# Two column halves for the small score products of a gated linear recurrence, and one address residue for three tiles

## The chip, the core and the metric

The kernel runs on one core of a Trainium2 chip. The metric is the device time of one execution in microseconds (us), the median of several runs. The core has five engines that run side by side and wait for each other through semaphores: PE (matrix products; its weight loads are shown as PEld), DVE and ACT (element-wise work and copies out of PSUM, the memory into which PE writes), POOL (element-wise work too, without access to PSUM) and SP, which here starts the transfers (DMAs).

A matrix product names a block of weights (up to 128 rows by 128 columns) and a moving block (128 rows by up to 512 columns). The number of weight columns is the number of partitions of PSUM that it writes. A product with 64 weight columns therefore writes either partitions 0 to 63 or 64 to 127; the text calls these the two column halves of the array.

## What is computed

One decoder layer on 2048 tokens of width 1024: a normalisation, a projection into two groups of heads, an output projection, a second normalisation, a gated MLP with a causal convolution of three taps, and a last normalisation. The change lies in the four heads of the first group, a linear recurrence with a decay for each channel:

```python
# S_t = diag(f_t) S_{t-1} + k_t v_t^T,  o_t = S_t^T q_t,  k_t = 1 - f_t
rel = b[:, :, :, None, :] - b[:, :, None, :, :]          # b: cumulative sum of log f
decay = jnp.exp(jnp.where(causal, rel, -jnp.inf))
scores = jnp.einsum('bhtk,bhsk,bhtsk->bhts', qi, ki, decay)
intra = jnp.einsum('bhts,bhsv->bhtv', scores, vi)
inter = jnp.einsum('bhtk,bhkv->bhtv', qi * jnp.exp(b), state)
new_state = state * jnp.exp(b_last)[...] + jnp.einsum('bhsk,bhsv->bhkv', ki * jnp.exp(b_last - b), vi)
```

The second group of heads is attention over a sliding window of 128 tokens, whose small products share PE with those of the recurrence.

## The kernel before

The tokens are worked in two halves of 1024. Each half goes through a mixing stage (heads of both groups), the output projection, gate and up projections of the MLP, and the down projection. Nearly all time goes to wide products, 128 by 128 weights on 512 columns, each of float32 data split into a high and a low part of a format that PE takes in one pass. In the trace such a product is one record. Small products of whole float32 data show as two records each (two pairs of weight load and product).

**Scores of the recurrence.** For each head, `hgrn` (L448) builds a tile `ST` of 8 chunks of 128 by 128 scores (row: the key's token s, column: the query's token t; zero unless s is not after t). It does so by levels. The diagonal (s = t) needs no decay: for each chunk one product of `K` and `q`, 128 by 128, goes to PSUM (`pdiag`, L473), four chunks to a bank, and DVE multiplies it by the identity tile `ident` on the way to `ST` (L474), which leaves the diagonal and writes zeros elsewhere. Then for m in 1, 2, 4, ..., 64 a level fills the blocks of m by m in which the query's block follows directly on the key's: keys s0 to s0+m, queries s0+m to s0+2m. Up to m = 16 one product serves two chunks and DVE copies its blocks under a mask (L502). At m = 32 and m = 64 each block is a product of its own of m by m (L515): the output starts at partition s0. At m = 32 there are two of these per chunk, at partitions 0 and 64; at m = 64 one, always at partition 0. ACT copies them into `ST` (L531), at m = 64 in one copy of 64 partitions by 8 chunks of 64.

**Output of the attention.** The products `poT` (L434) have 64 weight columns and 128 moving columns; the two heads that share a tile write partitions 0 to 63 and 64 to 127 in turn.

**The ring `ga`.** In the MLP stage two tiles with the tag `ga`, `GA` = 1056 floats wide, hold the gate's rows (1026 used). In the down projection `prep_piece` (L882) takes the same two tiles for the high and the low part of the weights of every third piece (`gad`, used at L929 to L931), and takes the ring `hi`/`lo` (4096 bytes each) for the others (`hid`, `lod`). A `ga` tile is 4224 bytes, so the second one starts 8 times 512 plus 128 bytes after the first.

**Order.** `ORDER` (L40) gives the order in which the stages are traced; a scheduler then sets the order of the instructions on each engine from its own cost estimates and from when buffers come free. So a change to one product moves others around it. Two PSUM banks with the tag `hg` are shared by `pdiag`, the levels, and the later small products of the recurrence.

Of the kernel before, what the change touches and what calls it, by code (L numbers as in the profile page):

```python
# [8 lines left out]
F32 = mybir.dt.float32  # L9
# [4 lines left out]
ALU = mybir.AluOpType  # L14
# [3 lines left out]
P = 128  # L18
# [5 lines left out]
TT = HALF // P  # L24
NB = HALF // 512
HG = 4
# [3 lines left out]
FT = FF // P  # L30
EPS = 1e-6
PIECES = [2, 2, 2, 2, 2, 1]
GA = 1056
OPS = ["B11", "T1", "B21", "T2", "T3", "B22", "T4"]
QUADS = ["A11", "A12", "A21", "A22"]
PRODUCTS = [("P1", "A11", "B11"), ("P5", "S1", "T1"), ("P6", "S2", "T2"), ("P3", "S4", "B22"),
# [13 lines left out]
def hymba_layer(ctx: ExitStack, tc: tile.TileContext, a: dict, out: bass.AP, rows_out: bass.AP):  # L50
    nc = tc.nc

    def pool(name, bufs=1, space=None, stack=ctx, **kw):
        if space is not None:
            kw["space"] = space
        return stack.enter_context(tc.tile_pool(name=name, bufs=bufs, **kw))

    cp = pool("const")
# [10 lines left out]
    def ps(kind, name):  # L69
        return spaces[kind].tile([P, 512], F32, tag=kind, name=name)  # L70
# [3 lines left out]
    def halves():  # L74
# [4 lines left out]
    nc.scalar.dma_start(nmw, a["norm_mix_w"])  # L79
    ones = cp.tile([P, P], F32, name="ones")  # L80
    nc.vector.memset(ones, 1.0)
    warm = cp.tile([P, 32], F32, name="warm")[:, 0:1]
    nc.scalar.activation(warm, ones[:, 0:1], AF.Sigmoid)
    ident = cp.tile([P, P], F32, name="ident")
    nc.gpsimd.memset(ident, 1.0)
    nc.gpsimd.affine_select(out=ident, in_=ident, compare_op=ALU.is_equal, fill=0.0,
                            base=0, pattern=[[-1, P]], channel_multiplier=1)
    state = cp.tile([P, HG, P], F32, name="state")
    halo = cp.tile([P, FT, 2], F32, name="halo")
    nc.vector.memset(halo, 0.0)  # L90
    kc = cp.tile([P, 2, P], F32R, name="kcarry")
# [172 lines left out]
    def slot(name):  # L264
        return hp.tile([P, HALF], F32, tag="m", name=name, bufs=KT)
# [52 lines left out]
    def across(t, base, dims):  # L318

        v = t[:, :]  # L320
        return bass.AP(v.tensor, v.offset + base, [list(v.ap[0])] + dims)

    def rows(kv):
        return slice(kv * HD, (kv + 1) * HD)
# [123 lines left out]
    def hgrn(hf, h, X, invb, vs, WG, gates, mix, p, fu=None):  # L448
# [8 lines left out]
        q = slot(f"hg{h}")  # L457
# [4 lines left out]
        K = p.tile([P, HALF], F32, tag="K", name="K", bufs=2)  # L462
# [3 lines left out]


        ST = p.tile([P, TT, P], F32, tag="t4", name="ST", bufs=2)
        for b in range(NB):
            pd = ps("hg", "pdiag")  # L470
            for i in range(4):
                c = slice((b * 4 + i) * P, (b * 4 + i + 1) * P)
                nc.tensor.matmul(pd[:, i * P:(i + 1) * P], K[:, c], q[:, c], start=True, stop=True)  # L473
            nc.vector.tensor_tensor(ST[:, 4 * b:4 * b + 4], pd.rearrange("p (i t) -> p i t", i=4),  # L474
                                    ident.unsqueeze(1).to_broadcast([P, 4, P]), op=ALU.mult)


        late = ORDER.index(f"p{h}") < ORDER.index(f"g{h}")
# [14 lines left out]
        for m in LEVELS:  # L493
            nb = HALF // (2 * m)
            pl = ps("hg", "plev")
            if m < 32:
                n, nu = 64 // m, TT // 2
                far, near = [[512 - m, 2], [P, nu], [2 * m, n], [1, m]], [[512 + m, 2], [P, nu], [2 * m, n], [1, m]]
                G = p.tile([P, 512], F32, tag="G", name="G", bufs=2)
                nc.scalar.copy(across(G, 0, [[m, 2], [P, nu], [2 * m, n], [1, m]]), across(K, 0, near))  # L500
                for u in range(nu):
                    marks[m] = nc.tensor.matmul(across(pl, u * 64, [[256, 2], [1, 64]]), G[:, u * P:(u + 1) * P],  # L502
                                                across(Q, u * P + m, [far[0]] + far[2:]), start=True, stop=True)
                nf = P // m
                Kv, Qv = across(K, 0, near), across(Q, m, far)
                Fk = across(F, 1, [[4 * nf - 1, 2], [nf, nu], [2, n], [0, m]])
                Fq = across(F, 0, [[4 * nf + 1, 2], [nf, nu], [2, n], [0, m]])
                nc.vector.tensor_tensor(Kv, Kv, Fk, op=ALU.mult)
                nc.vector.tensor_tensor(Qv, Qv, Fq, op=ALU.mult)
            else:  # L510
                Qv = Q.rearrange("p (b w m) -> p b w m", w=2, m=m)
                Kv = K.rearrange("p (b w m) -> p b w m", w=2, m=m)
                for c in range(TT):
                    for s0 in range(0, P, 2 * m):
                        nc.tensor.matmul(pl[s0:s0 + m, c * m:(c + 1) * m], K[:, c * P + s0:c * P + s0 + m],  # L515
                                         Q[:, c * P + s0 + m:c * P + s0 + 2 * m], start=True, stop=True)
                Fv = F.rearrange("p (b w) -> p b w", w=2)
                nc.vector.tensor_tensor(Qv[:, :, 1], Qv[:, :, 1], Fv[:, :, 0:1].to_broadcast([P, nb, m]), op=ALU.mult)
                nc.vector.tensor_tensor(Kv[:, :, 0], Kv[:, :, 0], Fv[:, :, 1:2].to_broadcast([P, nb, m]), op=ALU.mult)
            Fv = F.rearrange("p (b w) -> p b w", w=2)  # L520
            Fn = p.tile([P, max(nb, 16)], F32, tag=f"F{m}", name=f"F{m}", bufs=1)[:, 0:nb]
            nc.vector.tensor_tensor(Fn, Fv[:, :, 0], Fv[:, :, 1], op=ALU.mult)
            F = Fn
            if m < 32:
                mk = C.lmask[m].bitcast(U32).rearrange("p s t -> p (s t)")
                nc.vector.copy_predicated(across(ST.rearrange("p c t -> p (c t)"), m, far),
                                          across(mk, 0, [[64, 2], [0, nu], [m, n], [1, m]]),
                                          pl.rearrange("p (s u b m) -> p s u b m", s=2, u=nu, m=m))
                continue
            for s0 in range(0, P, 2 * m):  # L530
                nc.scalar.copy(ST[s0:s0 + m, :, s0 + m:s0 + 2 * m],  # L531
                               pl[s0:s0 + m, 0:TT * m].rearrange("p (c m) -> p c m", c=TT))
# [5 lines left out]
        for b in range(NB):  # L538
            pk = ps("hg", "pkn")
            n = min(4, kept - 4 * b)  # L540
            for i in range(n):
                c = slice((b * 4 + i) * P, (b * 4 + i + 1) * P)
# [3 lines left out]
        for b in range(NB):  # L546
            pu = ps("hg", "pu")
            for c in range(4 * b, min(4 * b + 4, kept)):
                i = c % 4
                marks["pu"] = nc.tensor.matmul(pu[:, i * P:(i + 1) * P], Kn[:, c], v[:, c], start=True, stop=True)  # L550
            for c in range(4 * b, min(4 * b + 4, kept)):
                i = c % 4
# [11 lines left out]
        for c in range(TT):  # L564
            cs = slice(c * P, (c + 1) * P)
            prev = state[:, h] if c == 0 else SS[:, c - 1]
            o = po[c // 4][:, c % 4 * P:(c % 4 + 1) * P]
# [205 lines left out]
    def gate_up(hf, ops, hs, nxt, p):  # L773
# [5 lines left out]
        for pr in range(FT // 2):  # L779
            f0 = 2 * pr  # L780
            W, nxt = nxt, None
            ga = [p.tile([P, GA], F32, tag="ga", name="ga", bufs=2)[:, 0:2 + HALF] for _ in range(2)]

# [300 lines left out]
    for hf in range(NH):  # L1084
        X, kv, invb, rs, f0 = nxt
        with ExitStack() as st:
            p = pool(f"mix{hf}", stack=st, reuse_waits="tile")
            KS, V = att_keys(hf, kv, invb, p)
            mix = [None] * KT
            vs = []  # L1090
            M, WG, gates = {}, {}, {}
            heads = [hgrn(hf, h, X, invb, vs, WG, gates, mix, p, None if h else f0) for h in range(HG)]
            pairs = [attend(hf, h, X, invb, KS, V, mix, p) for h in range(HG)]
            for name in ORDER:
                stage, n = name[:-1], int(name[-1])
                if stage in ("f", "q", "l", "s", "p"):
                    next(heads[n])
                elif stage in ("qa", "sc", "pv", "pw"):
                    next(pairs[n])
                elif stage == "g":  # L1100
                    gates[n]()
                elif stage == "w":
                    WG[n] = prep(a["w_g"][n])
                elif stage == "v":
                    vs += project_v(hf, n, X, rs, p)
                else:
                    M[n] = split(mix[n])
            M[7], M[3] = mix[7], mix[3]
        with ExitStack() as st:
            p = pool(f"ffn{hf}", stack=st, reuse_waits="tile")  # L1110
            kept, ops, hs, first = out_proj(hf, M, p)
            acts = gate_up(hf, ops, hs, first, p)
            nxt = down(hf, kept, acts, p)
# [69 lines left out]
```

## Time and profile before

| What | Before |
|---|---|
| device time, median of 3 runs | 2176.63 us (2175.63 to 2179.33) |
| the profiled execution: device time | 2176.63 us |
| the profiled execution: span, first to last instruction | 2174.6 us |
| busy share of the span: PE, PEld, DVE, ACT, POOL | 99%, 83%, 75%, 48%, 1% |
| granted clock of PE | 1.0 |
| matmul records | 11191 |

The span is 2.0 us shorter than the device time of the same execution. A row of the time line gives start and length in us, engine, source line, operation, output and inputs, shape, and how many equal instructions follow each other. Products overlap in their last part, so the length of one says little; what one costs PE is the distance from its start to the start of the next. The shape `128*64 128x64` means 128 rows by 64 weight columns, on 64 moving columns.

### The profile page before, as it was taken

The numbers are of one execution on the slowest core, as the hardware profiler recorded it, in microseconds if no ns is written. First come the engines' busy times: TensorE is split into PE (matmuls) and PEld (weight loads), VectorE is DVE, ScalarE is ACT, GpSimd is POOL, SyncE is SP. The second block draws the span as 40 slices with busy tenths as digits, with TensorE's granted clock in tenths as the row PEclk, the third lists the DMA queues.
The fourth block names the chain that finished last, engine by engine and source line by source line (L and its number), as shares of the span: only waits on it lengthen the run. The fifth ranks groups of instructions, "written<-read, shape, count | busy, mean of one in ns | idle before, by whom it ended". The sixth has DMA issues, their size and how long they took to land.

```text
span 2174.6 us, 28950 instructions
## 1 busy us (share of the span) xinstructions
PE 2158.8 (99%) x11191; PEld 1812.7 (83%) x11191; DVE 1624.5 (75%) x2429; ACT 1045.0 (48%) x1828; POOL 12.6 (1%) x37
## 2 busy tenths in 40 slices
PE   8999999999999999999999999999999999999998
PEld 7988988888888888888889889888888888888887
DVE  6566668689787888785765676677888888787865
ACT  6445455554444445345635365445644444443453
POOL 2000000000000000000000000000000000000000
PEclk9999999999999999999999999999999999999999
DMA  4111012413333234974641110114232323259743
GB/s 156 40 30 40 30 35 73 132 63 124 94 113 97 90 128 146 375 244 147 211 136 30 30 46 25 49 63 142 71 117 87 126 88 121 87 187 392 238 145 131
DMA packets 91145, 254.40 MB, mean 117 GB/s; under 512 B 11136, under 2 KB 13952, under 8 KB 91008
## 3 DMA queue, kind: packets, MB, share of 16 engines
q1 hardware_dynamic: 90576, 252.29, 34.8%
q8 instruction: 88, 1.44, 0.3%
q14 instruction: 49, 0.40, 0.1%
q10 hardware_dynamic: 432, 0.27, 0.0%
HBM read 195.37 MB, written 57.15 MB: 116 GB/s over the span
## 4 chain that ended last, share of the span: by engine, by line
PE 97%; DVE 1%; DMA 1%; ACT 1%; issue 0%; SPq 0%; DVEq 0%; ACTq 0%
PE pop L202 8%; PE X L742 7%; PE X L744 7%; PE X L743 7%; PE q L202 4%; PE hq L202 4%; PE g L202 4%; PE f L202 4%; PE Y L743 4%; PE Y L744 4%; PE Y L742 4%; PE pdx L931 3%; PE pdy L930 3%; PE pdx L930 3%; PE pdy L931 3%; PE pdx L929 3%
## 5 line engine op out<-in xcount | busy, mean ns | idle before, releaser
L617 ACT CAST whi<-raw 128x1024 fp32r<-128x1024 f32 x88 | 92.5, 1051 | 103.0 <-PE X L743 68.3
L813 DVE SCALAR_TENSOR_TENSOR y<-ga,cw,y 128x1024 f32<-128x1024 f32 x88 | 112.2, 1277 | 37.7 <-ACT y L811 37.7
L743 PE MATMUL X<-T,whi 128*128 128x512 f32 x352 | 136.9, 389 | 0.0
L742 PE MATMUL X<-T,whi 128*128 128x512 f32 x352 | 136.9, 389 | 0.0
L744 PE MATMUL X<-T,wlo 128*128 128x512 f32 x352 | 136.9, 389 | 0.0
L618 DVE TENSOR_TENSOR wlo<-raw,whi 128x1024 fp32r<-128x1024 f32 x88 | 107.0, 1216 | 5.6 <-ACT whi L617 5.6
L183 ACT CAST whi<-raw 128x1024 fp32r<-128x1024 f32 x58 | 60.5, 1048 | 98.0 <-PE g L202 20.1
L748 ACT COPY u<-X 128x512 f32<-128x512 f32 x88 | 51.6, 586 | 99.2 <-PE X L744 99.1
L618 DVE TENSOR_TENSOR xld<-raw,xhd 128x1024 fp32r<-128x1024 f32 x72 | 80.8, 1130 | 8.8 <-ACT xhd L617 8.5
L617 ACT CAST xhd<-raw 128x1024 fp32r<-128x1024 f32 x72 | 69.2, 976 | 33.7 <-DMA raw<-act0B 9.4
L202 PE MATMUL pop<-XH,wlo 128*128 128x512 f32 x256 | 83.7, 391 | 0.8 <-DVE wlo L184 0.8
L202 PE MATMUL pop<-XL,whi 128*128 128x512 f32 x256 | 83.8, 391 | 0.0
L202 PE MATMUL pop<-XH,whi 128*128 128x512 f32 x256 | 83.2, 396 | 0.2
L184 DVE TENSOR_TENSOR wlo<-raw,whi 128x1024 fp32r<-128x1024 f32 x58 | 70.2, 1215 | 12.5 <-ACT whi L183 12.5
L744 PEld LDWEIGHTS X<-T,wlo 128*128 128x128 f32 x352 | 66.1, 188 | 13.7
L743 PEld LDWEIGHTS X<-T,whi 128*128 128x128 f32 x352 | 66.1, 188 | 13.7
L742 PEld LDWEIGHTS X<-T,whi 128*128 128x128 f32 x352 | 66.1, 188 | 13.7
L748 ACT COPY s<-X 128x512 f32<-128x512 f32 x44 | 25.8, 587 | 106.5 <-PE X L744 106.5
L609 PE MATMUL pvv<-whi,XH 128*128 128x256 f32 x256 | 73.4, 288 | 0.0
L610 PE MATMUL pvv<-whi,XL 128*128 128x256 f32 x256 | 73.0, 287 | 0.0
L611 PE MATMUL pvv<-wlo,XH 128*128 128x256 f32 x256 | 72.4, 286 | 0.0
L742 PE MATMUL X<-T,Sh 128*128 128x512 f32 x176 | 68.7, 390 | 0.0
(391 smaller groups left out, 6532.1 us busy)
## 6 DMA issues: line engine op xcount, KB each, us to landing
wr<-in_w_down SPq DMA_DIRECT2D x90, 512.0 KB, 5.5
raw<-in_w_gate SPq DMA_DIRECT2D x44, 512.0 KB, 3.6
raw<-in_w_up SPq DMA_DIRECT2D x44, 512.0 KB, 3.7
raw<-act0T SPq DMA_DIRECT2D x20, 512.0 KB, 5.4
raw<-act1T SPq DMA_DIRECT2D x20, 512.0 KB, 4.9
act0B<-y SPq DMA_DIRECT2D x33, 256.0 KB, 2.3
act1B<-y SPq DMA_DIRECT2D x33, 256.0 KB, 2.2
raw<-in_w_out SPq DMA_DIRECT2D x16, 512.0 KB, 3.6
```

The lines of the kernel that those rows point to most:

```text
L202: nc.tensor.matmul(o[b], w, x[:, bs], start=f, stop=l)
L609: nc.tensor.matmul(o[:, 0:256], xh[:, t], hi[:, c], start=kt == 0, stop=False)
L610: nc.tensor.matmul(o[:, 0:256], xl[:, t], hi[:, c], start=False, stop=False)
L617: nc.scalar.copy(h, src)
L618: return (eng or nc.vector).tensor_tensor(l, src, h.bitcast(F32), op=ALU.subtract)
L742: nc.tensor.matmul(o, wh[:, ws], xh, start=i == 0 and not more, stop=False, skip_group_check=more)
L743: nc.tensor.matmul(o, wh[:, ws], xl, start=False, stop=False, skip_group_check=more)
L744: nc.tensor.matmul(o, wl[:, ws], xh, start=False, stop=i == 3, skip_group_check=more)
L748: nc.scalar.copy(t, o)
L813: nc.vector.scalar_tensor_tensor(y, g[:, w:w + HALF], C.cw[:, ft, w:w + 1], y, op0=ALU.mult, op1=ALU.add)
L930: nc.tensor.matmul(o, wh[:, i, c], al[:, i, cols], start=False, stop=False, skip_group_check=more)
L931: nc.tensor.matmul(o, wl[:, i, c], ah[:, i, cols], start=False, stop=l, skip_group_check=more)
```

## The change

Three things are changed.

1. The diagonal. A block of 64 by 64 tokens replaces the chunk of 128 by 128: 16 products per head in place of 8, each with 64 weight columns and 64 moving columns, the first half of a chunk to PSUM partitions 0 to 63 and the second to 64 to 127, in turn. All fit in one bank in place of two. DVE multiplies by the identity's two diagonal blocks, one instruction of 64 partitions by 512 for each half. The lower left quarter of each chunk, which the multiplication by the identity used to clear, is cleared by a memset on POOL.
2. Level 64. The 8 products per head write partitions 0 to 63 for even chunks and 64 to 127 for odd ones. ACT takes them out in two copies of 64 partitions by 256, the second from partitions 64 to 127 to partitions 0 to 63.
3. Addresses. `GA` becomes 1152 floats, 9 times 512 bytes, so both `ga` tiles start at the same residue of 512 bytes. `ident` and `state` are allocated ahead of the small tile `warm`. In the built program nearly all wide tiles stand at 192 bytes past a multiple of 512. Before the change, `ident` and the second `ga` tile stood at 320, the tiles `dd` and `fw` behind the ring at 448; after it all four stand at 192.

```diff
-GA = 1056
+GA = 1152
...
     nc.vector.memset(ones, 1.0)
+    ident = cp.tile([P, P], F32, name="ident")
+    state = cp.tile([P, HG, P], F32, name="state")
     warm = cp.tile([P, 32], F32, name="warm")[:, 0:1]
     nc.scalar.activation(warm, ones[:, 0:1], AF.Sigmoid)
-    ident = cp.tile([P, P], F32, name="ident")
...
-    state = cp.tile([P, HG, P], F32, name="state")
...
         ST = p.tile([P, TT, P], F32, tag="t4", name="ST", bufs=2)
-        for b in range(NB):
-            pd = ps("hg", "pdiag")
-            for i in range(4):
-                c = slice((b * 4 + i) * P, (b * 4 + i + 1) * P)
-                nc.tensor.matmul(pd[:, i * P:(i + 1) * P], K[:, c], q[:, c], start=True, stop=True)
-            nc.vector.tensor_tensor(ST[:, 4 * b:4 * b + 4], pd.rearrange("p (i t) -> p i t", i=4),
-                                    ident.unsqueeze(1).to_broadcast([P, 4, P]), op=ALU.mult)
+        nc.gpsimd.memset(ST[rows(1), :, 0:64], 0.0)
+        pd = ps("hg", "pdiag")
+        for c in range(TT):
+            for k in range(2):
+                ts = slice(c * P + k * 64, c * P + (k + 1) * 64)
+                nc.tensor.matmul(pd[rows(k), c * 64:(c + 1) * 64], K[:, ts], q[:, ts], start=True, stop=True)
+        for k in range(2):
+            r = rows(k)
+            nc.vector.tensor_tensor(ST[r, :, r], pd[r].rearrange("p (c t) -> p c t", t=64),
+                                    ident[r, r].unsqueeze(1).to_broadcast([64, TT, 64]), op=ALU.mult)
...
                 for c in range(TT):
                     for s0 in range(0, P, 2 * m):
-                        nc.tensor.matmul(pl[s0:s0 + m, c * m:(c + 1) * m], K[:, c * P + s0:c * P + s0 + m],
+                        o = pl[s0:s0 + m, c * m:(c + 1) * m] if m < 64 else pl[rows(c % 2), c // 2 * m:(c // 2 + 1) * m]
+                        nc.tensor.matmul(o, K[:, c * P + s0:c * P + s0 + m],
                                          Q[:, c * P + s0 + m:c * P + s0 + 2 * m], start=True, stop=True)
...
+            if m == 64:
+                for k in range(2):
+                    nc.scalar.copy(ST[0:m].rearrange("p (c k) t -> p c k t", k=2)[:, :, k, m:],
+                                   pl[rows(k), 0:TT // 2 * m].rearrange("p (c m) -> p c m", m=m))
+                continue
```

Since the scheduler works from the changed costs, the order on PE moves at many places of the mixing stage. Three of them show the kinds of moves. Lines of the changed kernel stand up to 9 further down (L473 becomes L474, L502 becomes L505, L515 becomes L519); `hg_533` and the like are the query tile of a head.

PE, first token half, head 0, the diagonal among the wide products `q` of the attention; before:

```order
L202 MATMUL q_657<-XL,whi 128x512
L202 MATMUL q_658<-XL,whi 128x512
L473 MATMUL pdiag<-hg_533,K 128x128 x8
L202 MATMUL q_657<-XH,wlo 128x512
L202 MATMUL q_658<-XH,wlo 128x512
```

and now:

```order
L202 MATMUL q_666<-XL,whi 128x512
L202 MATMUL q_667<-XL,whi 128x512
L474 MATMUL pdiag<-hg_533,K 64x64 x16
L505 MATMUL plev<-Q,G 128x2x64 x4
L202 MATMUL q_666<-XH,wlo 128x512
L202 MATMUL q_667<-XH,wlo 128x512
```

The first level, which stood 19 wide products further on as an interruption of its own, now follows the diagonal directly.

PE, first token half, head 2, where the diagonal meets the output products `poT` of an attention pair; before:

```order
L473 MATMUL pdiag<-hg_1920,K 128x128 x6
L434 MATMUL poT<-po,V 64x128
L434 MATMUL poT<-pp,V 64x128
L473 MATMUL pdiag<-hg_1920,K 128x128
L434 MATMUL poT<-pp,V 64x128
L434 MATMUL poT<-po,V 64x128 x2
```

and now:

```order
L474 MATMUL pdiag<-hg_1938,K 64x64 x7
L434 MATMUL poT<-po,V 64x128
L434 MATMUL poT<-pp,V 64x128
L474 MATMUL pdiag<-hg_1938,K 64x64 x2
L434 MATMUL poT<-pp,V 64x128
L434 MATMUL poT<-po,V 64x128 x2
```

The order is the same; what was an alternation of 128 and 64 weight columns is now one run of products with 64.

PE, first token half, head 3, where the diagonal meets the attention's scores `psc`; before:

```order
L473 MATMUL pdiag<-hg_2736,K 128x128 x6
L387 MATMUL psc<-KS,qh 128x128
L473 MATMUL pdiag<-hg_2736,K 128x128
L387 MATMUL psc<-KS,qh 128x256
L473 MATMUL pdiag<-hg_2736,K 128x128
L202 MATMUL g_3283<-XH,whi 128x512
```

and now:

```order
L474 MATMUL pdiag<-hg_2763,K 64x64 x8
L387 MATMUL psc<-KS,qh 128x128
L474 MATMUL pdiag<-hg_2763,K 64x64
L387 MATMUL psc<-KS,qh 128x256
L474 MATMUL pdiag<-hg_2763,K 64x64 x7
L505 MATMUL plev<-Q,G 128x2x64 x4
L202 MATMUL g_3319<-XH,whi 128x512
```

Here the narrow run is cut twice by products with 128 weight columns. The second token half has the same three pictures.

## The prediction, made before the changed kernel was run

> **What bounds the kernel now.** I read the page first: busy times, then the chain that ended last, then what PE waited for.
>
> ```profile
> span 2174.6 us, 28950 instructions
> PE 2158.8 (99%) x11191; PEld 1812.7 (83%) x11191; DVE 1624.5 (75%) x2429; ACT 1045.0 (48%) x1828; POOL 12.6 (1%) x37
> PE 97%; DVE 1%; DMA 1%; ACT 1%; issue 0%; SPq 0%; DVEq 0%; ACTq 0%
> ...
> PE kv L202 <- ACT XH L216: 6.3, 2, 5.4
> PE poT L434 <- DVE po L426: 1.0, 2, 0.5
> PE pop L202 <- DVE wlo L184: 0.8, 2, 0.4
> ```
>
> PE is busy for 99% of the span, the chain is PE for 97%, and of its waits 6.3 us lie at the start, where nothing changes; the others are of 1 us and less. So the time is the sum of what each product costs PE, plus about 8 us. A change is worth what it takes off the distance between the starts of products, wherever it stands, as long as DVE keeps up.
>
> **The price of a small product.** The time line of PE around head 0's diagonal:
>
> ```profile
> 61.13 0.61 PE L202 MATMUL q<-XL,whi 128*128 128x512 f32 x2
> 61.58 1.95 PE L473 MATMUL pdiag<-hg,K 128*128 128x128 f32 x16
> 63.28 0.71 PE L202 MATMUL q<-XH,wlo 128*128 128x512 f32 x2
> 63.83 0.62 PE L202 MATMUL q<-XH,whi 128*128 128x512 f32 x2
> 64.29 0.61 PE L202 MATMUL q<-XL,whi 128*128 128x512 f32 x2
> ```
>
> A pair of wide products takes 0.455 (61.13 to 61.58, 63.83 to 64.29). From 61.13 to 63.83 are 2.70 us with two such pairs in it, so the 16 records of the diagonal cost 1.79, or 0.112 each, and the interruption itself nothing that can be seen.
>
> Level 64 and level 32, with the wide products about them (the second row of each level is the same run, from an answer cut off earlier):
>
> ```profile
> 93.17 0.28 PE L611 MATMUL pvv<-wlo,XH 128*128 128x256 f32 x1
> 93.38 1.15 PE L515 MATMUL plev<-Q,K 128*64 128x64 f32 x16
> 94.80 0.28 PE L611 MATMUL pvv<-wlo,XH 128*128 128x256 f32 x1
> ...
> 93.38 0.56 PE L515 MATMUL plev<-Q,K 128*64 128x64 f32 x6
> ...
> 88.52 0.28 PE L609 MATMUL pvv<-whi,XH 128*128 128x256 f32 x1
> 88.73 0.70 PE L515 MATMUL plev<-Q,K 128*32 128x32 f32 x32
> 89.58 0.28 PE L611 MATMUL pvv<-wlo,XH 128*128 128x256 f32 x1
> 89.70 0.28 PE L609 MATMUL pvv<-whi,XH 128*128 128x256 f32 x1
> ...
> 88.73 0.51 PE L515 MATMUL plev<-Q,K 128*32 128x32 f32 x20
> ```
>
> Level 64, all in one column half: 10 more records take 1.15 − 0.56 = 0.59, so 0.059 each. Level 32, alternating between partitions 0 and 64: 12 more take 0.70 − 0.51 = 0.19, so 0.016 each, two in 0.032. A wide `pvv` product takes 0.12 (89.58 to 89.70). From 93.17 to 94.80 are 1.63; without three steps of 0.12 that is 1.27, of which 16 × 0.059 = 0.94 are the records. The rest, **0.33, is the price of going to narrow weights and back**; level 32 gives 1.18 − 0.36 − 0.51 = 0.31.
>
> Do two halves really run at once, with 64 columns? The output products of the attention alternate in the same way. First all of one run by a window on L434 (length, PE busy, records, then PEld), then rows of its time line:
>
> ```profile
> 131.03:132.71 1.68, 1.67 (x26) 1.50 (x26) 1.00 0.00 0
> ...
> 131.42 0.27 PE L434 MATMUL poT<-po,V 128*64 128x128 f32 x1
> 131.42 0.38 PE L434 MATMUL poT<-pp,V 128*64 128x128 f32 x2
> 131.64 0.27 PE L434 MATMUL poT<-pp,V 128*64 128x128 f32 x1
> 131.64 0.38 PE L434 MATMUL poT<-po,V 128*64 128x128 f32 x2
> ```
>
> Two records start at 131.42, two at 131.64 (and two between): two in 0.11, where one with 128 moving columns alone takes 0.112. 26 in a row would be 2.9 us; the run took 1.67. So a pair costs what one does, and I take 0.059 for a pair of 64 by 64. The bounds are 0.032 (level 32's pair, half as wide) and 0.118 (one after the other).
>
> The Trainium skill says otherwise in one place ("TensorE: Matmul & The Clock Gate", Part 3, what overlaps and what doesn't): a weight load overlaps a running product only when their row groups differ. Here all products use all 128 rows, so by that rule the halves would go in turn with the loads exposed. The `poT` rows above speak against it; it is the third rival below.
>
> **The sum**, against the profiled execution's own 2176.63 us (span 2174.6 and 2.0 around it; it is also the median of the three runs).
>
> 1. *Diagonal*: 64 products of two records, 128 × 0.112 = 14.3 us. Now 128 products, 64 pairs of products, 128 pairs of records: 128 × 0.059 = 7.6. **−6.7** (between −10.2 and +0.8).
> 2. *Level 64*: 128 × 0.059 = 7.6 becomes 64 pairs, 3.8. **−3.8** (between −5.5 and 0).
> 3. *Going narrow and back*: the diagonal was 128 wide and is now 64. Counted in PE's order before and after, runs of narrow products go from 55 to 63: heads 0 and 1 add one each, head 3 three (cut twice by `psc`), head 2 saves one net since its diagonal now joins the two `poT` runs. 8 × 0.33 = **+2.6**.
> 4. *Interruptions of the wide products*: 202 become 191 in PE's order, as the first level now stands right behind the diagonal. The interruption above cost nothing within itself; the first wide pair behind it took 0.55 in place of 0.455 (63.28 to 63.83), part of it weight load that the last small product had already given back. So between 0 and 0.1 each: **−0.5** (−1.1 to 0).
> 5. *Addresses.* The groups of the down projection, same operation and shape, by ring:
>
> ```profile
> L929 PE MATMUL pdx<-xhd,gad 128*128 128x512 f32 x96 | 37.4, 389 | 0.0
> L930 PE MATMUL pdx<-xld,gad 128*128 128x512 f32 x96 | 38.0, 395 | 0.0
> L931 PE MATMUL pdx<-xhd,gad 128*128 128x512 f32 x96 | 37.2, 397 | 0.0
> L930 PE MATMUL pdx<-xld,hid 128*128 128x512 f32 x168 | 65.4, 389 | 0.0
> L931 PE MATMUL pdx<-xhd,lod 128*128 128x512 f32 x168 | 63.4, 389 | 0.0
> L742 PE MATMUL Y<-B,dd 128*128 128x512 f32 x8 | 3.1, 389 | 0.0
> ...
> 877.73 0.39 PE L929 MATMUL pdx<-xhd,gad 128*128 128x512 f32 x1
> 881.20 0.39 PE L929 MATMUL pdx<-xhd,gad 128*128 128x512 f32 x1
> ...
> 872.07 0.39 PE L929 MATMUL pdx<-xhd,hid 128*128 128x512 f32 x1
> 875.47 0.39 PE L743 MATMUL X<-T,whi 128*128 128x512 f32 x1
> ```
>
> With `ga` weights the products at L930 and L931 are 6 and 8 ns longer than with the ring `hi`/`lo`; at L929 they are not. While L930 runs, the low part is loaded, and L931 multiplies by it: both touch the second `ga` tile, the one that stands 128 bytes off the others. The tile `dd`, 256 off, shows 389. So the offset of 128 is the suspect. In starts: 15 products from 877.73 to 881.20 take 3.47, 15 without `ga` from 872.07 to 875.47 take 3.40, so 0.0047 per product; with 96 triples in `pdx`, 80 in `pdy` and 2 × 16 with the `xh2d` operands there are 624 products: **−2.7**, estimated (0 to −3).
> The same for `ident`: 335 transposes of 128 columns, a quarter of the width, so at most about 2 ns each, 0.7 either way. I take 0.
> 6. *Off PE.* DVE: two instructions of 512 elements per partition before and now. ACT: one copy more per head; POOL: a memset per head, four times as long per partition as those of the profile:
>
> ```profile
> L474 DVE TENSOR_TENSOR ST<-pdiag,ident x16: 682/692/693, 62.7 to 1412.2; 128x512 f32<-128x512 f32 x16
> L531 ACT COPY ST<-plev x24: 344/363/581, 89.5 to 1447.4; 32x256 f32<-32x256 f32 x16, 64x512 f32<-64x512 f32 x8
> L113 POOL MEMSET lmask<- 128x128 f32 x5 | 1.0, 204 | 0.0
> ...
> 350.00:370.00 20.00, 19.16 (x170) 16.39 (x169) 17.12 (x34) 10.77 (x44) 0.00 (x0) 1.00 0.06 23
> 1420.00:1450.00 30.00, 29.07 (x228) 25.06 (x227) 27.00 (x50) 15.90 (x52) 0.00 (x0) 1.00 0.15 49
> ```
>
> Two copies of 256 at 0.36 in place of one at 0.58 are 0.14 more per head on an engine that is busy for 48%; uncovered, 1.1 in all. The memset is about 0.8 (4 × 0.204) on an idle POOL with nothing queued behind it. DVE's first masked copy into `ST` waits for it, and behind that the products `K` and `Q` of the next level; it becomes free to run with the same buffer for which DVE waited before, and PE's diagonal runs meanwhile. Uncovered it would be 6.5. I take 0 for both.
> 7. *Waits.* The last two rows (length, then busy PE, PEld, DVE, ACT, POOL) are the end of each mixing stage: DVE is busy for 17.1 of 20 and 27.0 of 30 us, and PE is short of work for 0.8 and 0.9. DVE gets no less to do there, and PE comes sooner. **+0.5** (0 to +4).
>
> −6.7 − 3.8 + 2.6 − 0.5 − 2.7 + 0.5 = −10.6: **2166.0 us**.
>
> **The rivals.**
>
> *The addresses do nothing*: the 6 and 8 ns come from something else about the ring, say its two parts lying in one tag. For it: the trace shows no address. Against it: `hid`/`lod` are loaded in the same rhythm, and only the second tile's products are slow. Without step 5: 2168.7.
>
> *DVE becomes the bound at the end of the mixing stages.* For it: the two windows. Against it: in the windows before them it has slack, and the gain of head 3, next to the end, is only a quarter of 7.9 (steps 1 to 3), 1 us per half. If PE loses all of that and as much again to a later DVE, +3 to +4 on step 7: 2169.4.
>
> *The halves do not run at once for 64 by 64, and it gets slower.* The place is each narrow run; with pairs at p, steps 1 and 2 give 192 p against 21.9. Without the addresses' help, and with +2.6 of step 3 and steps 4 and 7 cancelling, break-even is p = 19.3 / 192 = 0.100. From there on it is slower; at 0.118 it is +3.4 without step 5 (2180) and about +0.7 with it (2177.3). Against it: `poT` and level 32, which both alternate in the same way.
> By the Trainium skill's rule on row groups the loads would stand between the products too: the `poT` run's loads, 1.50 us for 26 or 0.058 each, make it 384 × 0.117 = 45 us for 21.9, and with step 3 about 2202.
>
> *More than forecast*: interruptions worth 0.1 each and no new waits, 2164.
>
> **Chances and numbers.** Forecast 0.60 (of its own 2164.5 to 2167.5); addresses nothing 0.13; DVE 0.15; more than forecast 0.05; in turn with the addresses' help, no change, 0.04; in turn and slower 0.03, the rule's case 0.01 of it. The range from 2163 to 2171 holds the first four and leaves out the two with halves in turn and the far end of the DVE case. A measurement of this kernel tells about 0.2%, 4.4 us, from no change: all of the first four are beyond that but for the DVE case's far end. Faster 0.91, same 0.06, slower 0.03.
>
> **What will show it.** Level 64's run should take about 0.61 us to the next start in place of 1.08, a diagonal run alone 1.08 in place of 1.79, with starts in pairs. Records of `gad` should all show 389. PE's waits at `poT` and level 32 at the ends of the mixing stages show step 7. I am wrong if starts come singly 0.059 apart, if PE idles for more than 4 us more at the ends of the mixing stages, or if the memset is what DVE waits for.

## The result, and the profile after

The changed kernel takes **2168.17 us** (median of 7 runs, 2167.45 to 2171.08) where the kernel before, beside it, takes 2176.01 (2175.59 to 2179.33): ratio 0.9962, 95% interval 0.9953 to 0.9972. The forecast was 2166.0, with a range from 2163 to 2171. The two profiled executions are 2176.63 and 2167.45, the spans 2174.6 and 2165.7, 8.9 us apart; the medians are 7.8 apart. Run again later, the changed kernel took 2169.77 beside 2176.32 (0.9970, 0.9958 to 0.9981).

The page of the changed kernel, its first rows, the chain and what PE waited for (us in total, times, longest):

```profile
span 2165.7 us, 29275 instructions
PE 2148.0 (99%) x11319; PEld 1801.6 (83%) x11319; DVE 1624.0 (75%) x2429; ACT 1046.9 (48%) x1836; POOL 20.7 (1%) x45
PE 97%; DVE 2%; DMA 0%; ACT 0%; issue 0%; SPq 0%; DVEq 0%; ACTq 0%
...
PE kv L202 <- ACT XH L216: 6.0, 2, 5.6
PE poT L434 <- DVE pp L426: 2.5, 3, 1.2
```

PE still sets the time, and its busy time is 10.8 us shorter with 128 more records (64 more products of two records each). What is new is the second wait: 2.5 us at `poT`, 1.0 before. DVE stands in the chain with 2% in place of 1%.

The groups that the change touches (busy us, mean ns of one, idle before):

```profile
L474 PE MATMUL pdiag<-hg,K 128*64 128x64 f32 x256 | 11.5, 226 | 0.0
L519 PE MATMUL plev<-Q,K 128*64 128x64 f32 x128 | 5.6, 227 | 0.0
L530 DVE COPY_PREDICATED ST<-lmask,plev 128x512 f32<-128x512 uint32 x40 | 38.3, 957 | 0.3
L939 PE MATMUL pdx<-xld,gad 128*128 128x512 f32 x96 | 37.3, 389 | 0.0
L940 PE MATMUL pdx<-xhd,gad 128*128 128x512 f32 x96 | 36.4, 389 | 0.0
```

The `gad` products of the last two rows, at 395 and 397 ns before, are at 389 like those at L938. DVE idles 0.3 us in all ahead of the masked copies that wait for POOL's memset, so that one is covered.

The diagonal of head 0 and its level 64 in the time line of PE (start, length to the last end, line, number of records):

```profile
60.86 0.61 PE L202 MATMUL q<-XL,whi 128*128 128x512 f32 x2
61.40 1.15 PE L474 MATMUL pdiag<-hg,K 128*64 128x64 f32 x32
62.48 0.95 PE L505 MATMUL plev<-Q,G 128*128 128x128 f32 x6
...
91.80 0.28 PE L618 MATMUL pvv<-whi,XH 128*128 128x256 f32 x1
92.01 0.69 PE L519 MATMUL plev<-Q,K 128*64 128x64 f32 x16
92.62 0.39 PE L619 MATMUL pvv<-whi,XL 128*128 128x256 f32 x1
```

From 61.40 to 62.48 are 1.08 for the whole diagonal, from 92.01 to 92.62 are 0.61 for level 64: the two numbers that the prediction named as its test.

Where the 8.9 us of the two spans lie shows a sum over the whole trace: for each product the distance from its start to the start of the next one on PE, grouped by what the product is. The table gives the difference to the kernel before in us, for the changed kernel and for four kernels that make only a part of the change (the first four experiments). A wait counts with the product that stands ahead of it.

| products | before | after | addresses alone | halves alone | diagonal alone | level 64 alone |
|---|---|---|---|---|---|---|
| diagonal | 14.28 | -4.49 | 0 | -4.49 | -4.49 | 0 |
| levels 1 to 16 | 33.02 | +1.14 | 0 | +1.14 | +1.13 | 0 |
| `poT`, `ppt` | 51.80 | -1.47 | 0 | -1.46 | -1.48 | +0.06 |
| other small, wide ones of the mixing stages | 738.6 | +0.52 | -0.15 | +0.84 | +0.49 | +0.21 |
| level 64 | 8.53 | -3.03 | 0 | -3.03 | 0 | -3.05 |
| level 32 (with the wait behind it) | 6.21 | +1.32 | 0 | +1.32 | +1.31 | 0 |
| `gad` | 144.3 | -2.73 | -2.73 | 0 | 0 | 0 |
| `kv` at the start, rest of the feed-forward | 1165.8 | -0.90 | -0.62 | -0.15 | -0.59 | -1.20 |
| all | 2162.5 | -9.63 | -3.50 | -5.85 | -3.59 | -3.99 |

The last group but one is chance: its products are the same in all six kernels, and in a second profile of the changed kernel it stood at +0.63. In that second execution PE's granted clock (the figure behind POOL) stands at 0.50 for 3.4 us of this group, and the products there cost 1.6 us more in all:

```profile
1093.90:1097.30 3.40, 3.40 (x9) 2.69 (x9) 1.96 (x14) 1.05 (x1) 0.00 (x0) 0.50 0.23 89
```

The first profiles of the six kernels have no such stretch ahead of the last product. Three later ones have it at the end of the second mixing stage, behind PE's wait at `poT`: the changed kernel with `GA` at 1088 and at 1120, and the diagonal on quarters. In the first two the group of `poT` and `ppt` is 1.0 and 1.2 us longer than in the changed kernel, with the same order of products. Apart from this the other groups repeat to 0.1 us or so, and the parts add up to within 0.2. To the span come 0.1 more at the start and 0.6 more behind the last product.

### The profile page after: what moved, and what is told of

Read it like the earlier page. It is cut to its first block, busy times and chain, and to the rows that moved or that the text cites. A ratio compares the mean times of both kernels' runs of the same rounds, so it can differ in the third digit from the quotient of the medians.

```text
span 2165.7 us, 29275 instructions
## 1 busy us (share of the span) xinstructions
PE 2148.0 (99%) x11319; PEld 1801.6 (83%) x11319; DVE 1624.0 (75%) x2429; ACT 1046.9 (48%) x1836; POOL 20.7 (1%) x45
## 3 DMA queue, kind: packets, MB, share of 16 engines
q8 instruction: 89, 1.46, 0.3%
## 4 chain that ended last, share of the span: by engine, by line
PE 97%; DVE 2%; DMA 0%; ACT 0%; issue 0%; SPq 0%; DVEq 0%; ACTq 0%
PE X L751 7%; PE X L753 7%; PE X L752 7%; PE pop L202 7%; PE q L202 4%; PE g L202 4%; PE hq L202 4%; PE f L202 4%; PE Y L753 4%; PE Y L752 4%; PE Y L751 4%; PE pdx L938 3%; PE pdx L939 3%; PE pdx L940 3%; PE pdy L939 3%; PE pdy L940 3%
## 5 line engine op out<-in xcount | busy, mean ns | idle before, releaser
L626 ACT CAST xhd<-raw 128x1024 fp32r<-128x1024 f32 x72 | 69.3, 978 | 34.9 <-DMA raw<-act0B 10.6
```

Of the source, the lines that this page charges most:

```text
L626: nc.scalar.copy(h, src)
```

## The experiments

**The parts of the change, each alone.** Four kernels between before and after. *Addresses alone* is the kernel before with these lines:

```diff
-GA = 1056
+GA = 1152
     ones = cp.tile([P, P], F32, name="ones")
     nc.vector.memset(ones, 1.0)
+    ident = cp.tile([P, P], F32, name="ident")
+    state = cp.tile([P, HG, P], F32, name="state")
     warm = cp.tile([P, 32], F32, name="warm")[:, 0:1]
     nc.scalar.activation(warm, ones[:, 0:1], AF.Sigmoid)
-    ident = cp.tile([P, P], F32, name="ident")
...
-    state = cp.tile([P, HG, P], F32, name="state")
```

> Only the addresses of the changed kernel: the second ga tile, dd and ident stand at the same residue as the first; the column halves are left as before. The theory (step 5): gad records at L930 and L931 fall from 395 and 397 to 389 ns, 624 products at 0.0047 less, 2.7 us off the kernel before (about 2173.5 where it takes 2176.2). The rival (the addresses do nothing, the 6 and 8 ns come from the rhythm of the loads and vanished with the new order of the products): the records stay at 395 and 397 and the time within 0.5 us of the kernel before.

Measured: 2173.61 (11 runs) beside 2176.36, ratio 0.9988 (0.998 to 0.9997).

```profile
L930 PE MATMUL pdx<-xld,gad 128*128 128x512 f32 x96 | 37.3, 389 | 0.0
L931 PE MATMUL pdx<-xhd,gad 128*128 128x512 f32 x96 | 36.4, 389 | 0.0
```

These are the two slow groups of `gad` in this kernel, whose order of products is that of the kernel before. Both are as fast as the others now, and the table gives 2.73 us for 624 products. The place in memory is the cause; the rival falls. The transposes by `ident`, which was moved too, stay within 0.03 us per group (`ppt`, `pkn`, `pot`): its place is worth nothing, as the prediction took it.

*Halves alone* is the changed kernel with the old `GA` and the old order of `ident` and `state`:

> Only the column halves of the changed kernel: diagonal and level 64 as in it, the addresses as before. The theory (steps 1 to 4 and 7): -6.7 - 3.8 + 2.6 - 0.5 = -8.4 on PE, of which 1 to 2 come back as waits at poT at the ends of the mixing stages: -6 to -7 against the kernel before, gad records at 395 and 397. The rival on the addresses: -8 to -9 as in the changed kernel, with gad records at 389.

Measured: 2171.84 (11 runs) beside 2176.36, ratio 0.9981 (0.9972 to 0.999); the `gad` groups show 395 and 397 again. By the medians it is 4.5, by PE's starts 5.85, short of the 6 to 7 expected.

*Diagonal alone* takes into the kernel before only the new loop at `pdiag`, its memset and its two products by `ident`; *level 64 alone* only this and the two copies that belong to it:

```diff
-                        nc.tensor.matmul(pl[s0:s0 + m, c * m:(c + 1) * m], K[:, c * P + s0:c * P + s0 + m],
+                        o = pl[s0:s0 + m, c * m:(c + 1) * m] if m < 64 else pl[rows(c % 2), c // 2 * m:(c // 2 + 1) * m]
+                        nc.tensor.matmul(o, K[:, c * P + s0:c * P + s0 + m],
```

> The kernel before with the new diagonal alone; level 64 in one half, old addresses. The theory (steps 1, 3 and 4): -6.7 + 2.6 - 0.5 = -4.6, a diagonal run that stands alone 1.08 us to the next start. A rival for the going narrow (that it costs nothing, 0 in place of 0.33 a run): -7.2. If the waits at poT come with the diagonal: up to 1.5 less gain, and the page lists 2.5 us of them as in the changed kernel.

> The kernel before with level 64 alternating between the halves alone; diagonal 128 wide, old addresses. The theory (step 2): 16 records in 0.61 us to the next start in place of 1.08, -3.8 if all of it reaches the end, since no run is added and DVE has the same to do. If DVE bounds the place where level 64 stands in heads 2 and 3: only -2 to -3, and PE's waits grow by as much.

Measured: diagonal alone 2173.51 (11 runs), ratio 0.9989 (0.998 to 0.9998); level 64 alone 2174.01 (11 runs), ratio 0.9989 (0.9981 to 0.9998). Of PE's waits, `poT` with the diagonal alone:

```profile
PE poT L434 <- DVE pp L426: 2.5, 3, 1.2
```

and with level 64 alone, with one that is new there:

```profile
PE poT L434 <- DVE po L426: 1.0, 2, 0.5
...
PE pop L202 <- ACT XH L444: 0.2, 1, 0.2
```

The new wait at `poT` comes with the diagonal, not with level 64. Level 64's own gain is smaller than 8 x 0.46: six of its runs go from 1.075 to 0.615 us to the next start, but behind the two of head 3 PE runs into a wait, in the first half one of 0.07, too short for the list (0.756 to the next start), in the second half the second row above, which leaves its run at 1.04 as before. In size that is near the second theory's case, 3.05 of 3.8, but the engine that PE waits for there is ACT and not DVE.

**Does the alternation make the pair?** The changed kernel, with the diagonal's two loops swapped:

```diff
-        for c in range(TT):
-            for k in range(2):
+        for k in range(2):
+            for c in range(TT):
                 ts = slice(c * P + k * 64, c * P + (k + 1) * 64)
```

> The changed kernel with the diagonal's two loops swapped: the same 256 records, but first all of the lower column half and then all of the upper one, so that neighbours no longer alternate. The theory (a pair of halves runs in the time of one product only because neighbours write different halves): records 0.059 apart as in level 64 of the kernel before, 256 x 0.059 = 15.1 in place of 7.6, +7.5 us against the changed kernel and about the time of the kernel before. The rival (a 64 by 64 product is cheap by itself, or the two halves go in turn anyway): a run still 1.08 us long, no change.

Measured: 2173.49 (11 runs) beside 2177.56, ratio 0.9984 (0.9975 to 0.9993). The time line of PE at the same place:

```profile
62.19 1.90 PE L474 MATMUL pdiag<-hg,K 128*64 128x64 f32 x32
64.02 0.72 PE L505 MATMUL plev<-Q,G 128*128 128x128 f32 x4
```

The same 32 records take 1.83 in place of 1.08, and the sum over the diagonals is 5.48 us higher than in the changed kernel; all other groups but the chance one stay within 0.15. So neighbours in different column halves run at once, and neighbours in one half go in turn, 0.059 each. The rule of the Trainium skill that the prediction weighed ("TensorE: Matmul & The Clock Gate", Part 3, what overlaps and what doesn't) does not hold for these products: they share all row groups, and the pair costs what one does. The table "Why this matters for your kernels" on the same page of the Trainium skill has the other side of it, small outputs put on distinct column groups to run together; that agrees with 1.08 against 1.83. The expected 7.5 was too high. A run of 32 strictly in turn would take 0.107 for its first record, 30 x 0.059, and 0.152 for its last, 2.03 in all; level 64 of the kernel before has the same two ends and 14 x 0.059 between them, 1.075. The run here takes 1.83, since near its middle, where the lower half gives way to the upper, three pairs of records start only 4 to 7 ns apart. The alternating run has the same ends: 16 x 0.059 = 0.94, and 0.14 on top.

**Which distance costs?** The changed kernel with other values for `GA`: 1040 puts the second `ga` tile 64 bytes off the first modulo 512 and `dd` 128 off, 1088 puts them 256 and 0 off, 1120 puts them 384 and 256 off.

> The changed kernel with the second ga tile 64 bytes off the residue of the first, modulo 512 (128 off before, 0 now), and dd 128 off. If any step off the residue costs the same: gad records at L939 and L940 at 395 and 397 ns. If it is the 128 itself, and dd with it: gad at 389, and dd (8 records, 256 off before and at 389) above 389. The rival, that the offset is not the cause: all 389.

> The changed kernel with the second ga tile 256 bytes off the residue of the first, modulo 512, and dd at the residue itself. By the row of dd in the kernel before, which stood 256 off and showed 389 ns: gad records at 389 throughout. If any offset but 0 costs: 395 and 397 at L939 and L940.

> The changed kernel with the second ga tile 384 bytes off the residue of the first modulo 512, dd at 256 off. After the offsets of 64 and 128 cost 2 to 9 ns per product and 256 nothing, a rule modulo 256 expects gad records at L939 and L940 at 395 and 397 ns, as for 128, and dd at 389. A rule modulo 512 of the distance alone (384 is as far as 128 from the next 512) expects the same; that only small positive offsets cost, 389 throughout.

Their groups, 64 first, with `dd`:

```profile
L939 PE MATMUL pdx<-xld,gad 128*128 128x512 f32 x96 | 37.6, 391 | 0.0
L940 PE MATMUL pdx<-xhd,gad 128*128 128x512 f32 x96 | 37.1, 397 | 0.0
...
L751 PE MATMUL Y<-B,dd 128*128 128x512 f32 x8 | 3.2, 396 | 0.0
```

256:

```profile
L939 PE MATMUL pdx<-xld,gad 128*128 128x512 f32 x96 | 37.3, 389 | 0.0
L940 PE MATMUL pdx<-xhd,gad 128*128 128x512 f32 x96 | 36.4, 389 | 0.0
```

and 384:

```profile
L939 PE MATMUL pdx<-xld,gad 128*128 128x512 f32 x96 | 38.0, 395 | 0.0
L940 PE MATMUL pdx<-xhd,gad 128*128 128x512 f32 x96 | 37.2, 397 | 0.0
...
L751 PE MATMUL Y<-B,dd 128*128 128x512 f32 x8 | 3.1, 389 | 0.0
```

64, 128 and 384 cost, 0 and 256 do not; and `dd`, a tile of quite another stage, turns slow in the one kernel where it stands 128 off. All that was seen fits a rule modulo 256. Whether the distance from the other tile counts, or the second tile's own place, no run separates: the other tiles stayed where they were. Each was run once; by PE's starts their `gad` products take 0.2, 2.7 and 0.0 us less than in the kernel before.

**Is DVE what PE waits for at the end of the mixing stage?** The time line of PE in the changed kernel, at the last head of the first half:

```profile
358.52 1.04 PE L423 MATMUL ppt<-ident,sc 128*128 128x128 f32 x8
359.49 0.70 PE L519 MATMUL plev<-Q,K 128*32 128x32 f32 x32
361.37 1.05 PE L434 MATMUL poT<-po,V 128*64 128x128 f32 x7 [1.18 <-DVE pp L426]
```

and DVE there:

```profile
358.72 0.69 DVE L512 TENSOR_TENSOR Q<-Q,F 128x512 f32<-128x512 f32 x1
359.33 0.73 DVE L530 COPY_PREDICATED ST<-lmask,plev 128x512 f32<-128x512 uint32 x1
359.95 0.68 DVE L426 TENSOR_TENSOR po<-ppt,ownT 128x512 f32<-128x512 f32 x1
360.54 0.68 DVE L426 TENSOR_TENSOR pp<-ppt,prevT 128x512 f32<-128x512 f32 x1
361.14 0.68 DVE L426 TENSOR_TENSOR po<-ppt,ownT 128x512 f32<-128x512 f32 x1
```

In the kernel before PE did the same work in another order there:

```profile
361.25 0.60 PE L423 MATMUL ppt<-ident,sc 128*128 128x128 f32 x4
361.69 1.06 PE L502 MATMUL plev<-Q,G 128*128 128x128 f32 x8
362.58 0.60 PE L423 MATMUL ppt<-ident,sc 128*128 128x128 f32 x4
363.32 0.41 PE L434 MATMUL poT<-po,V 128*64 128x128 f32 x2
363.90 0.70 PE L515 MATMUL plev<-Q,K 128*32 128x32 f32 x32 [0.17 <-DVE Q L509]
365.12 0.54 PE L434 MATMUL poT<-po,V 128*64 128x128 f32 x5 [0.52 <-DVE po L426]
```

Before, half of the transposes `ppt` stood ahead of level 16, and DVE did half of `po` and `pp` before it came to level 16's Q (363.16). Now all eight stand behind it, and DVE has Q, the masked copy and the first products by the masks to do one after the other before `poT` may start. The test takes one of these instructions away:

```diff
             if m < 32:
                 mk = C.lmask[m].bitcast(U32).rearrange("p s t -> p (s t)")
+                if h == 3 and m == 16:
+                    continue
                 nc.vector.copy_predicated(across(ST.rearrange("p c t -> p (c t)"), m, far),
```

> The changed kernel without one instruction of DVE per half: head 3's masked copy of level 16 into ST is left out, so the scores of that level are missing in head 3. PE's order is the same. The theory (at the ends of the mixing stages DVE, not PE, sets when poT can start, and part of the gain went there): the time from level 32 of head 3 to the next start falls from 1.88 us by DVE's 0.6 to about 1.28 in each half, PE's wait at poT from 2.5 to about 1.3, the time by about 1.2. The rival (PE waits for ACT's exponentials or for the transposes, DVE is only the last name on the list): no change.

Measured: 2168.30 (5 runs) beside 2177.56, ratio 0.9958 (0.9946 to 0.9971). The medians cannot tell 1.2 us from the changed kernel; the time line can:

```profile
360.00 0.70 PE L519 MATMUL plev<-Q,K 128*32 128x32 f32 x32
361.27 1.05 PE L434 MATMUL poT<-po,V 128*64 128x128 f32 x7 [0.57 <-DVE pp L426]
```

From level 32 to `poT` it is 1.27 in place of 1.88, the same in the second half, and the group of level 32 in the sum falls by 1.22. The 0.6 us of DVE ahead of `po` are 0.6 us of PE. DVE sets the start of `poT`, and the rival falls. That it is the new place of the transposes that made this wait longer, and not only that PE comes sooner, is argued from the two time lines; no run puts the old order into the changed kernel.

Behind level 64 of the same head the wait is another. The output projection `pop` starts at 364.45 in the changed kernel, where level 64 has run from 363.67; what ends just before is a cast on ACT, which could start only when `poT` was done:

```profile
363.81 0.59 ACT L444 CAST XH<-poT 128x512 fp32r<-128x512 f32 x1 [1.26 <-PE poT L434]
...
364.45 0.73 PE L202 MATMUL pop<-XH,whi 128*128 128x512 f32 x2
```

Level 64 is work that PE does meanwhile; a shorter level 64 does not bring `pop` forward. No run shortens this cast, so that part rests on the time line.

**Further in the same direction.** First the changed kernel again, for its runs on the same chip and its longer end.

> The changed kernel once more, for the runs beside it on the same chip. The theory: 8 us below the kernel before, 2168 where that takes 2176; PE's distances as in its first profile (diagonal runs 1.08, level 64 0.61, level 32 of head 3 1.88 us to the next start), the end behind the last product 7.2 to 7.3 us again. If the longer end (0.6 more than in the kernel before) was a chance of one execution: 6.7.

Measured: 2169.77 as told above; PE's groups within 0.1 us of the first profile (the last but one, `kv` and the feed-forward, 1.5 more, by the stretch at half the clock), and 7.26 us from PE's last start to the end of the span. The longer end repeats.

Then four column quarters in place of two halves, for the diagonal (blocks of 32 tokens) and for level 32:

```diff
-        nc.gpsimd.memset(ST[rows(1), :, 0:64], 0.0)
+        nc.gpsimd.memset(ST, 0.0)
...
-            for k in range(2):
-                ts = slice(c * P + k * 64, c * P + (k + 1) * 64)
-                nc.tensor.matmul(pd[rows(k), c * 64:(c + 1) * 64], K[:, ts], q[:, ts], start=True, stop=True)
+            for k in range(4):
+                ts = slice(c * P + k * 32, c * P + (k + 1) * 32)
+                nc.tensor.matmul(pd[k * 32:(k + 1) * 32, c * 32:(c + 1) * 32], K[:, ts], q[:, ts], start=True, stop=True)
...
+                        if m < 64:
+                            r0 = s0 + 32 * (c % 2)
+                            o = pl[r0:r0 + m, c // 2 * m:(c // 2 + 1) * m]
...
```

DVE then has four instructions of 32 partitions in place of two of 64, and ACT twice as many copies at level 32.

> A further step of the changed kernel: the diagonal from blocks of 32 tokens on four column quarters (64 records a run), and level 32 on four quarters where it alternated between two. The theory that column groups run at once, carried on to four: four records in the 0.032 us that two take now, 0.008 each, a diagonal run 0.43 and a level 32 run 0.25 shorter, 8 of each: -5.4 us against the changed kernel. The rival (a record is not issued faster than every 0.016 us): level 32 as before, the diagonal 64 x 0.016 = 1.02 in place of 0.94, so +0.7 us; with DVE's four smaller instructions in place of two and more narrow work between, 0 to +2.

> Only the diagonal of that further step on four quarters, level 32 left on two. By four at once: -3.4 us against the changed kernel, a run alone 0.65 in place of 1.08 us to the next start. By one record per 0.016: +0.7, a run 1.16.

Measured: quarters 2166.40 (5 runs), ratio 0.9954 (0.994 to 0.9967); the diagonal alone on quarters 2168.83 (5 runs), 0.9964 (0.9952 to 0.9977); the changed kernel beside them 0.9970. The time line of PE with quarters, diagonal and level 32 of head 0:

```profile
62.17 0.76 PE L474 MATMUL pdiag<-hg,K 128*32 128x32 f32 x64
62.86 0.83 PE L505 MATMUL plev<-Q,G 128*128 128x128 f32 x5
...
87.72 0.46 PE L523 MATMUL plev<-Q,K 128*32 128x32 f32 x32
88.10 0.39 PE L626 MATMUL pvv<-wlo,XH 128*128 128x256 f32 x1
```

64 records in 0.69 and 32 in 0.38 us to the next start (on two halves the diagonal took 1.08 and level 32 0.63): four run at once, and no limit of one record per 0.016 us shows. The diagonals give 3.0 us and level 32, with the wait behind it, another 1.9, a little less than expected (3.4 and 2.0), but the medians only 3.4. PE's waits in and behind the mixing stages grow, and here it is ACT that they name; in the changed kernel its waits for ACT other than `kv` were 0.2:

```profile
PE poT L434 <- DVE pp L426: 1.6, 2, 1.4
PE pop L202 <- ACT XH L444: 1.3, 2, 1.1
PE po L584 <- ACT on L587: 1.0, 2, 0.5
PE poT L434 <- DVE m L405: 0.9, 1, 0.9
```

The diagonal alone on quarters misses its forecast: its diagonals give the same 3.0 us, but its median lies only 0.9 below the changed kernel's, where 3.4 were expected. It has the same new waits for ACT (0.9 and 1.0), and its profile also the stretch at half the clock.

The kernel with both on quarters is the fastest of all that ran, 9.9 us below the kernel before by medians. The intervals of the two ratios overlap, but on this chip its slowest run (2167.79) is faster than the fastest of the changed kernel beside it (2168.84).

## Why the prediction held, step by step

- *Steps 1, 3 and 4, diagonal, narrowing, interruptions* (-6.7, +2.6, -0.5, together -4.6): in the kernel with the diagonal alone the first four groups of the table, which are all that they touch but for the wait, give -4.49 + 1.13 - 1.48 + 0.49 = -4.35. The sum of the three is right to 0.3, and the rival by which going narrow costs nothing (-7.2) falls; the three terms one by one no run separates. The price per pair, 0.059 for two of 64 by 64, is right: with neighbours in one half the same records go in turn.
- *Step 2, level 64* (-3.8): a run goes from 1.075 to 0.615, 0.46; eight are 3.7. PE got 3.03 of it. The 0.65 that is missing is a wait behind head 3's runs and belongs to step 7.
- *Step 5, addresses* (-2.7): -2.73, with the order of the products unchanged. It was found from three groups of the same shape that differed by 6 and 8 ns.
- *Step 6, off PE* (0): PE waits nowhere for the memset, ACT's copies or DVE's new form.
- *Step 7, waits* (+0.5): **the step that was mis-sized.** It measured +1.32 behind level 32 and +0.65 behind level 64 of head 3, +2.0 in all, about 1.0 in each half. That is the gain of head 3, which the second rival priced at 1 us per half and saw lost with as much again on top. The first part of that rival happened, the second did not, and only the 1.32 is a wait for DVE: the 0.65 is one for ACT's cast, which step 7 did not have. The prediction looked at how busy DVE is in these windows; it should have followed the chains from level 16 over DVE to `poT`, and from `poT` over ACT to `pop`, instruction by instruction, in the changed order. That the transposes now stand in one piece behind level 16 could be read from the order before the run.
- *Left out of the sum*: the end behind the last product, +0.6 (below).

So PE's sum, without the chance group, is -4.35 - 3.7 - 2.73 + 2.0 = -8.8, where the table has -8.7 and the forecast -10.6. With the chance group's -0.9, and 0.7 back at both ends, this makes the 8.9 of the two spans. By the number alone the prediction was less good than by its rows: the median of 2168.17 lies in the range but outside the forecast's own 2164.5 to 2167.5, and nearest to the 2168.7 of the rival in which the addresses do nothing, which the rows refute. Of the rivals, the one that kept the time unchanged or slower (halves in turn) is refuted by the swapped loops: in turn the diagonal alone would have cost 5.5 us more.

## What to carry to other kernels

Where PE is the bound and a product's output has at most half of the 128 columns, write neighbours into different column halves or quarters: here they ran at once, and it is the order of neighbours that decides, so an inner loop over the halves is all that it needs. Where groups of one shape differ by a few ns, compare the addresses of the weight tiles; 4.4 ns on average over 624 products were nearly a third of this gain. And when PE gets faster, add up the instructions of the next engine between what PE hands over and what it takes back, in the changed order: DVE's busy share of 86% and a cast on an ACT that is busy for 48% hid two chains that together took back a whole head's gain.

## What the runs showed that was not expected

- *The place of weight tiles*: with the second `ga` tile 64, 128 or 384 bytes off, two of the three products of `gad` cost 2 to 8 ns more each, at 256 none; `dd`, which stood 0, 128 and 256 off, was slow at 128 alone. What in the chip does it, no run shows.
- *Four at once*: 64 records of 32 by 32 on four column quarters in 0.69 us, where 32 of 64 by 64 on two halves take 1.08.
- *The ends of a narrow run*: whether in turn or alternating, the first step of a run that stands alone is 0.107 and the last 0.152, where a step inside is 0.059, so each such run costs 0.14 beyond its records.
- *Half the clock for 3.4 us*: ahead of the last product no profile of the first six kernels has such a stretch, five of the later eight profiles do, one of them twice. What it costs depends on where it falls (1.6 us in `kv`, 1.0 and 1.2 in `poT`); why it comes in some executions and not in others, no run shows.
- *The end of the kernel*: from PE's last start to the end of the span it is 6.7 us in the kernel before and with the addresses alone, and 7.2 to 7.3 in all twelve profiles with new halves, with level 64 alone as well. The last transfers were issued 0.27 slower by ACT's queue in the changed kernel; here in the kernel before:

```profile
2170.94 0.86 ACTq L1059 DMA_DIRECT2D rows<-y  x2
```

and in the changed one:

```profile
2161.45 1.13 ACTq L1068 DMA_DIRECT2D rows<-y  x2
```

The instructions there are the same. This row is not the reason: with the diagonal alone it is 0.86 as before, and the end is 7.16 all the same. In the eleven profiles with POOL's new memset 0.5 lies on POOL: from the end of the instruction with which it clears the semaphores to the end of the span it is 0.77 to 0.80, in the kernel before and with the addresses alone 0.29. With level 64 alone, which has no memset, it is 0.29 too, and there the last transfer lands 0.47 later. That the memset is the cause is not shown.
